# Mamba-2 stage: the masked B·C product held in PSUM, small sums in the banks of the transposes, and one tile's state input made by VectorE

## The chip, the cores and the metric

The kernel runs on one core of a Trainium2 chip. The core has a matrix engine (PE, TensorE), three engines for element-wise work (DVE = VectorE, ACT = ScalarE, POOL = GpSimd), and a queue that issues the transfers (SP, SyncE). The engines run their own instruction streams in order, and wait for one another through semaphores. Matmuls write to PSUM, eight banks of 128 x 512 fp32; everything else lies in SBUF. The metric is the time of one execution on the device in microseconds (us), lower is better. Before the change three runs took 1116.57, 1116.24 and 1118.81 us, a median of 1116.57.

## What is computed

One step of a two-layer recurrent decoder, for a prompt of 512 tokens and for eight samples of one token each, with the same weights. Layer 0 joins gated DeltaNet and gated linear attention. Layer 1, the only one that the change touches, is a Mamba-2 SSD block: 32 heads of width 64 in 4 groups, each group with one B and one C row of 128 numbers a token.

```python
def odd_layer(h, conv_buf, s_ssd, pre_g, post_g, w_in, conv_w, conv_b, dt_bias, a_log, d_skip, norm_g, w_out):
    u = rmsnorm(h, pre_g)
    z, xbc, dt = _split(einsum('bld,de->ble', u, w_in), ODD_SPLITS)
    xbc, new_buf = causal_conv(xbc, conv_buf, conv_w, conv_b)
    xs, Bm, Cm = _split(xbc, (SSD_DI, SSD_G * SSD_N, SSD_G * SSD_N))
    dt = softplus(dt + dt_bias)
    y, s_new = ssd_chunked(xs, dt, -exp(a_log), Bm, Cm, s_ssd)
    y = (y + d_skip[:, None] * xs) * silu(z)
    y = rmsnorm(y in 4 groups of 512, norm_g)
    return h + rmsnorm(y @ w_out, post_g), new_buf, s_new

def ssd_chunked(x, dt, A, Bm, Cm, h0):
    xdt, lam = x * dt[..., None], cumsum(dt * A)           # within a chunk
    m = einsum('nbtgs,nbjgs->nbgtj', Cm, Bm) * exp(lam_t - lam_j)   # for j <= t, else 0
    y = einsum('nbgktj,nbjgkp->nbtgkp', m, xdt) + exp(lam_t) * (C . state)
    state = exp(lam_last) * state + sum_j exp(lam_last - lam_j) * B_j x xdt_j
```

## The kernel before

**Stages.** The program computes layer 0, its output projection, the SSD block (from about 690 to 1050 us of the profiled execution) and its output projection. The Python code is a list of operations in the order of the algorithm; a scheduler deals them anew to each engine by its own model of their times, so the order in which an engine runs them isn't that of the text, and a small edit can move many rows. Tiles come from pools with a fixed number of buffers by tag: a new tile waits until the readers of the tile that had its buffer are done. Each PSUM tag has its own banks: pj 2, po 1, pf 1, pr 2, px 1, ps 1, eight in all. `bank(tag)` (L128) hands them out.

**A group of the SSD block** (`ssd_group`, four calls) has the same steps each time. All arrays are transposed: 128 features on the partitions, 512 tokens in four chunks of 128 along the free axis.

- B and C are projected (matmuls L267 to L269, three to a product because fp32 is split in two parts) and convolved (`conv`, DVE's products `stt`, L148, in bank pf). B is transposed by PE (L1232, a pr bank) and copied by ACT to `btk`, a tile of tag kqg. The products of B and C of each chunk (L1237) go to bank po; DVE multiplies them with the triangular mask `tri` into `cbm`, another kqg tile (`tt`, L145, in the trace kqg<-po,tri).
- The samples' B and C rows are transposed (L1245, bank ps), copied by ACT, written to DRAM (`bd`) and broadcast from there over all partitions into four tiles of tag inv (in the trace inv<-bd). `bcv` (matmul L1259, bank ps) is B·C of each sample.
- For each of four tiles j (two heads): x and the gate are projected and convolved; x is transposed (L1321, a pr bank); x times dt is made from PSUM into `xdt`, by DVE for tiles 0 to 2 (ch<-pr,c) and by eight scalings of ACT (L1328) for tile 3; POOL multiplies that with the decay to the chunk's end, `xdc`, into `xd[j]`, the input of the state (ap<-ch,c). For each head ACT makes the decay matrix (L1343, L1344), and DVE multiplies it with `cbm` (dec<-dec,kqg). The matmuls L1348 make y of the tile from both.
- With the tiles go the samples: `sample_x` and `sample_state(j)`, in which POOL multiplies the state by the broadcast C and B (sb<-inv,st and sb<-inv,smh), DVE reduces (L1285) and adds, and ACT scales the state (L1290). The samples of the last group are kept until after the stage.
- The states of the four chunks (L1361, pr banks) need `btk` and all four `xd`. Then, for each tile, the state's share of y (L1390) is scaled by DVE in PSUM (po<-po,pre), added, and multiplied with the gate; ACT squares, POOL adds the squares into `acc`. PE sums them by column (L1402, bank ps), DVE reads these sums (L1404), POOL takes the power -0.5 (smc), PE broadcasts the result over the partitions (L1410, `rs`, bank ps), and four products of DVE (L148, of<-of,vhalf,ps) scale y with it.

**What sets the order around the change.** The bank ps, of which there is one, serves in turn L1245, L1259, the column sums L1402 and `rs` (L1410), and in groups 1 and 3 the sum in `sample_norm` (L1217). The two pr banks serve the transposes of B and x, the states, and half of the L1390 products. Bank po serves L1237, L1348 and the other half of L1390.

Of the kernel before, what the change touches and what calls it, by code (L numbers as in the profile page):

```python
# [14 lines left out]
MULT, ADD, SUB, MIN, MAX, POW = ALU.mult, ALU.add, ALU.subtract, ALU.min, ALU.max, ALU.pow  # L15

P = 128
# [7 lines left out]
C = 128  # L25
NC = TP // C
# [5 lines left out]
SG = 4  # L32
# [25 lines left out]
def kernel(  # L58
# [45 lines left out]
    act, dve, pool, pe = nc.scalar, nc.vector, nc.gpsimd, nc.tensor  # L104
# [12 lines left out]
    phase = [0]  # L117
# [3 lines left out]
    def sb(shape, dt=F32, tag="f1"):  # L121
        uid[0] += 1
        return wrk.tile(shape, dt, name=f"{tag}_{uid[0]}", tag=tag, bufs=BUFS[tag])

    def const(shape, name, dt=F32):
        return cst.tile(shape, dt, name=name)

    def bank(tag):  # L128
        uid[0] += 1
        if tag == "po":  # L130
            tag = ("po", "pf")[npo[0] % 2 if phase[0] < 2 else 0]
            npo[0] += 1
        return psm.tile([P, 512], F32, name=f"{tag}_{uid[0]}", tag=tag, bufs=PBUFS[tag])
# [4 lines left out]
    def c4(ap):  # L138
        return ap.rearrange("p (c t) -> p c t", c=NC)
# [4 lines left out]
    def tt(eng, out, a, b, op):  # L144
        eng.tensor_tensor(out, a, b, op=op)  # L145
# [4 lines left out]
    def chunk(c):  # L150
        return slice(c * C, (c + 1) * C)
# [215 lines left out]
    start = ExitStack()  # L367
# [28 lines left out]
    tri = tri1.unsqueeze(1).to_broadcast([P, NC, P])  # L396
# [131 lines left out]
    ps = bank("pr")  # L528
# [8 lines left out]
    ps = bank("pr")  # L537
# [650 lines left out]
    ps = bank("pr")  # L1188
    for c in range(NC):
        pe.transpose(ps[:, chunk(c)], sd[:, chunk(c)], ident)  # L1190
    dtl = lay1[:, 0:256].rearrange("p (c h) -> p c h", c=NC)
    act.activation(dtl, c4(ps)[:, :, 0:64], AF.Copy)
    lamc = dtl[:, :, 32:64]
    ps = bank("pr")
# [3 lines left out]
    xdc = sb([P, NC, SH], tag="c5")  # L1198
    act.activation(slast, pv, AF.Exp)
    tt(dve, xdc, pv, lamc, SUB)  # L1200
    act.activation(xdc, xdc, AF.Exp)
    tailo = sb([P, 11, 24], tag="tail")
    ysm = sb([P, 16, NS], tag="c5")
    zsm = sb([P, 16, NS], tag="c5")
# [20 lines left out]
    def ssd_group(g):  # L1225
# [3 lines left out]
        b_, c_ = bcm  # L1229
        ps = bank("pr")  # L1230
# [1 line left out]
            pe.transpose(ps[:, chunk(c)], b_[:, chunk(c)], ident)  # L1232
        btk = sb([P, NC, C], tag="kqg")
        act.activation(btk, c4(ps), AF.Copy)
        ps = bank("po")
        for c in range(NC):
            pe.matmul(ps[:, chunk(c)], b_[:, chunk(c)], c_[:, chunk(c)], start=True, stop=True)  # L1237
        cbm = sb([P, NC, C], tag="kqg")
        tt(dve, cbm, c4(ps), tri, MULT)

        bcs = sb([P, 2, NS], tag="sms")
        conv_samples(tailo, cvw[1], hpo, 16 + g, 2, 4, bcs)
        ps = bank("ps")
# [14 lines left out]
        ps = bank("ps")  # L1258
# [48 lines left out]
        yt, xd, gts = [], [], []  # L1307
        for j in range(4):
            pr = 4 * g + j
            h0 = 2 * pr  # L1310
            x_ = sb([P, T], tag="kq")
            gt = conv_gate(o_w_in[0], (O_X + pr * P, pr * P), u1, pr, cvw[1], hpo, tailo, x_, pr == 15)
            pool.tensor_copy(zsm[:, pr], gt[:, TP:T])
            gts.append(gt)
            if j % 2 == 1:
                sample_x(j // 2)
            if j > 1:
                samples(j - 2)
            ps = bank("pr")
            for c in range(NC):  # L1320
                pe.transpose(ps[:, chunk(c)], x_[:, chunk(c)], ident)  # L1321
            sh = [P, NC, 2, 64]
            xdt = sb([P, NC, 2, 64], tag="ch")
            px = ps.rearrange("p (c h e) -> p c h e", c=NC, h=2)
            na = 4 if j == 3 else 0
            for c in range(na):
                for hh in range(2):
                    act.activation(xdt[:, c, hh], px[:, c, hh], AF.Copy, scale=dtl[:, c, h0 + hh:h0 + hh + 1])  # L1328
            if na < NC:
                tt(dve, xdt[:, na:], px[:, na:], dtl[:, na:, h0:h0 + 2].unsqueeze(3).to_broadcast([P, NC - na, 2, 64]), MULT)  # L1330
            xd.append(sb([P, NC, P], tag="ap"))
            tt(pool, xd[j].rearrange("p c (h e) -> p c h e", h=2), xdt,
               xdc[:, :, h0:h0 + 2].unsqueeze(3).to_broadcast(sh), MULT)

            po = bank("po")
            rbs = []
            for hh in range(2):
                h = h0 + hh
                rb = sb([P, TP], tag="dec")
                rbs.append(rb)  # L1340
                dma(rb, ldr[h:h + 1, :].to_broadcast([P, TP]))
                for c in range(NC):
                    act.activation(rb[:, chunk(c)], rb[:, chunk(c)], AF.Relu, scale=-1.0, bias=lamc[:, c, h:h + 1])  # L1343
                act.activation(rb, rb, AF.Exp, scale=-1.0)  # L1344
                tt(dve, c4(rb), c4(rb), cbm, MULT)
            for c in range(NC):
                for hh in range(2):
                    pe.matmul(po[hh * 64:hh * 64 + 64, chunk(c)], xdt[:, c, hh, :], rbs[hh][:, chunk(c)], start=True, stop=True)  # L1348
            yt.append(sb([P, T], tag="of"))
            y = yt[j][:, 0:TP]  # L1350
            stt(y, x_[:, 0:TP], dcol[:, pr:pr + 1], po, MULT, ADD)
# [5 lines left out]
        h0 = 8 * g  # L1357
        for c in range(NC):
            ps = bank("pr")
# [3 lines left out]
            if c:  # L1363
                sh = [P, 8, 64]
# [40 lines left out]
        tt(pool, rc, rc, nhalf[:, 0:NC], POW)  # L1405
        dg = sb([P, NC, C], tag="dec")
        tt(dve, dg, ident.unsqueeze(1).to_broadcast([P, NC, C]), bc3(rc, C), MULT)
        rs = bank("ps")
        for c in range(NC):
            pe.matmul(rs[:, chunk(c)], ones, dg[:, c, :], start=True, stop=True)  # L1410
        for j in range(4):
# [60 lines left out]
```

## Time and profile before

| | |
|---|---|
| median of three runs | 1116.57 us |
| the profiled execution | 1120.96 us |
| its span, from first to last instruction | 1119.2 us |
| mean clock granted to TensorE | 0.972 of full speed |
| SSD stage | about 690 to 1050 us |

The profile is one execution, recorded by the hardware. Its span leaves out 1.8 us around the program. A group of instructions is named by its line, engine, operation and tiles (`dec<-dec,kqg` is a product written to a dec tile from a dec and a kqg tile), followed by shapes, the count, busy time, mean time of one, and the idle time of the engine ahead of it with what ended it. A row of the timeline has its start, its length, the engine, the line, the instruction, and in brackets the idle time ahead. A row of the view by stretches has, for each engine (PE, its weight loads PEld, DVE, ACT, POOL), the busy time and the number of instructions, then the granted clock, the share of the DMA engines and the bytes moved (GB/s).

### The profile page before, as it was taken

How to read it: one execution, taken by the hardware profiler on the slowest of the kernel's cores; microseconds unless marked ns; L12 is line 12 of the kernel's file. 1: busy time of each engine (PE TensorE's matmuls, PEld its weight loads, DVE VectorE, ACT ScalarE, POOL GpSimd, SP SyncE). 2: the span in 40 equal slices, each digit the busy share in tenths (PEclk: the TensorE clock that was granted, in tenths of full speed). 3: DMA queues.
4: the chain of work that ended last, by engine and by line, in shares of the span. 5: the costliest groups of instructions: out<-in, count | busy, mean ns of one | idle time of the engine just before them, and what ended most of it. 6: DMA issues, size and time to landing. Idle time of an engine off the chain costs nothing.

```text
span 1119.2 us, 23031 instructions
## 1 busy us (share of the span) xinstructions
PE 1048.8 (94%) x8900; PEld 1006.4 (90%) x8900; DVE 720.3 (64%) x1207; ACT 627.4 (56%) x1518; POOL 535.7 (48%) x701
## 2 busy tenths in 40 slices
PE   8999979999989989999889999998999999999997
PEld 7999979899989989889888988898998988989997
DVE  5798353655867754565645366698787688778543
ACT  5566445544444645546233465775686676775452
POOL 4034961304124377114435362386469477468632
PEclk8999999999999989989998999999999999999999
DMA  5234245622554424745563351755657556657632
GB/s 166 81 92 110 72 139 153 194 59 78 171 145 124 110 70 130 217 137 146 160 197 115 100 170 39 210 146 144 188 170 198 181 161 194 206 177 216 187 90 78
DMA packets 241732, 160.01 MB, mean 143 GB/s; under 512 B 21463, under 2 KB 221358, under 8 KB 241606
## 3 DMA queue, kind: packets, MB, share of 16 engines
q1 hardware_dynamic: 241622, 158.53, 48.9%
q8 instruction: 70, 1.15, 0.4%
q14 instruction: 40, 0.33, 0.1%
HBM read 127.05 MB, written 31.84 MB: 142 GB/s over the span
## 4 chain that ended last, share of the span: by engine, by line
PE 40%; DMA 17%; POOL 15%; DVE 13%; ACT 8%; issue 4%; SPq 2%; DVEq 0%; POOLq 0%; ACTq 0%
PE pj L267 9%; PE pj L268 9%; PE pj L269 9%; POOL sb L145 6%; POOL st L145 3%; ACT dec L1343 2%; DVE w L145 2%; DMA sb<-ud 2%; DMA st<-in_state_ssd_dram 2%; DMA out_dram<-st 2%; DVE f L148 1%; DMA pre<-ldr 1%; POOL w L145 1%; DMA inv<-bd 1%; PE px L268 1%
## 5 line engine op out<-in xcount | busy, mean ns | idle before, releaser
L267 PE MATMUL pj<-ua,w 128*128 128x256 f32 x776 | 228.3, 295 | 4.5 <-ACT ua L342 1.7
L269 PE MATMUL pj<-ua,w 128*128 128x256 f32 x776 | 226.9, 293 | 1.2 <-DVE w L145 1.2
L267 PE MATMUL pj<-ub,w 128*128 128x264 f32 x768 | 226.5, 295 | 1.4 <-ACT ub L342 0.9
L269 PE MATMUL pj<-ub,w 128*128 128x264 f32 x768 | 225.7, 294 | 0.0
L268 PE MATMUL pj<-ub,w 128*128 128x264 f32 x742 | 219.0, 295 | 0.0
L268 PE MATMUL pj<-ua,w 128*128 128x256 f32 x750 | 217.7, 291 | 0.0
L145 DVE TENSOR_TENSOR w<-raw,w 128x1024 fp32r<-128x1024 f32 x102 | 136.2, 1335 | 62.9 <-PE pj L268 33.9
L267 PEld LDWEIGHTS pj<-ua,w 128*128 128x128 f32 x776 | 151.3, 195 | 7.4 <-ACT ua L342 2.0
L251 ACT ACTIVATE w<-raw 128x1024 fp32r<-128x1024 f32 x123 | 130.0, 1057 | 46.9 <-DMA raw<-in_o_w_out_dram 11.1
L269 PEld LDWEIGHTS pj<-ua,w 128*128 128x128 f32 x776 | 151.5, 195 | 3.1 <-DVE w L145 1.4
L267 PEld LDWEIGHTS pj<-ub,w 128*128 128x128 f32 x768 | 148.2, 193 | 2.6 <-ACT ub L342 1.1
L269 PEld LDWEIGHTS pj<-ub,w 128*128 128x128 f32 x768 | 148.1, 193 | 1.8 <-issue 1.5
L268 PEld LDWEIGHTS pj<-ua,w 128*128 128x128 f32 x750 | 146.7, 196 | 0.2
L268 PEld LDWEIGHTS pj<-ub,w 128*128 128x128 f32 x742 | 143.3, 193 | 1.6 <-issue 1.1
L145 POOL TENSOR_TENSOR w<-raw,w 128x1024 fp32r<-128x1024 f32 x20 | 49.7, 2484 | 49.1 <-PE px L268 19.4
L145 POOL TENSOR_TENSOR sb<-inv,st 128x512 f32<-128x512 f32 x32 | 54.3, 1714 | 22.7 <-DMA inv<-bd 13.7
L148 DVE SCALAR_TENSOR_TENSOR pf<-xr,cvw,pf 128x512 f32<-128x512 f32 x72 | 54.0, 750 | 11.6 <-ACT pf L440 10.7
L148 DVE SCALAR_TENSOR_TENSOR f<-xr,cvw,f 128x512 f32<-128x512 f32 x72 | 57.6, 799 | 4.3 <-ACT f L440 3.6
L145 POOL TENSOR_TENSOR sms<-sms,sms 128x16 f32<-128x16 f32 (+2 forms) x56 | 22.1, 396 | 77.0 <-ACT sms L960 41.9
L1290 ACT ACTIVATE st<-st,c 128x128 f32<-128x128 f32 x128 | 41.1, 395 | 24.6 <-POOL sb L145 24.6
L439 ACT ACTIVATE xr<-pj 128x256 f32<-128x256 f32 (+1 forms) x72 | 27.3, 380 | 36.7 <-PE pj L269 36.5
L1343 ACT ACTIVATE dec<-dec,c 128x128 f32<-128x128 f32 x128 | 40.5, 390 | 9.8 <-DMA dec<-ldr 8.6
(600 smaller groups left out, 2819.5 us busy)
## 6 DMA issues: line engine op xcount, KB each, us to landing
raw<-in_e_w_in_dram SPq DMA_DIRECT2D x56, 512.0 KB
raw<-in_o_w_in_dram SPq DMA_DIRECT2D x40, 512.0 KB
out_dram<-st SPq DMA_DIRECT2D x32, 512.0 KB
raw<-in_e_w_out_dram SPq DMA_DIRECT2D x32, 256.0 KB
st<-in_state_ssd_dram SPq DMA_DIRECT2D x16, 512.0 KB
dec<-ldr SPq DMA_DIRECT2D x32, 256.0 KB
raw<-in_o_w_out_dram SPq DMA_DIRECT2D x32, 256.0 KB
sb<-vd SPq DMA_DIRECT2D x8, 512.0 KB
```

The costliest lines, as they stand in the source:

```text
L145: eng.tensor_tensor(out, a, b, op=op)
L148: dve.scalar_tensor_tensor(out, a, s, b, op0=op0, op1=op1)
L251: act.activation(wh, rv, AF.Copy)
L267: pe.matmul(ps, wh, uh[b], start=(k == 0), stop=False)
L268: pe.matmul(ps, wh, ul[b], start=False, stop=False)
L269: i0 = pe.matmul(ps, wl, uh[b], start=False, stop=(k == NK - 1))
L439: act.activation(hsl(xr[:, 3:3 + T], b), halves[b], AF.Copy)
L1290: act.activation(st[:, b], st[:, b], AF.Copy, scale=sc2[:, 1, pr, b:b + 1])
L1343: act.activation(rb[:, chunk(c)], rb[:, chunk(c)], AF.Relu, scale=-1.0, bias=lamc[:, c, h:h + 1])
```

## The change

Four edits, all within the SSD stage.

1. `cbm` stays in PSUM. The products of B and C are written to bank ps, through a new tag "pc", and masked in place by DVE; bank po and one kqg tile are no longer used for it, and the mask products dec<-dec,cbm read one operand from PSUM.
2. Everything in the stage that asked for bank ps (L1245, L1259, the column sums L1402, the sum of `sample_norm`) now takes a pr bank.
3. `rs`, the broadcast of the norm, is put into bank po.
4. `xdl`, dt times `xdc` for heads 6 and 7 of each group, is made once by POOL; the state input of tile 3 is made by DVE from the transposed x in PSUM and `xdl`, instead of by POOL from `xdt` and `xdc`. ACT's eight scalings stay, since y needs `xdt`.

```diff
     def bank(tag):
         uid[0] += 1
+        if tag == "ps" and phase[0] == 2:
+            tag = "pr"
+        if tag == "pc":
+            tag = "ps"
...
     act.activation(xdc, xdc, AF.Exp)
+    xdl = const([P, NC, 8], "xdl")
+    tt(pool, xdl.rearrange("p c (g h) -> p c g h", g=SG), xdc.rearrange("p c (g h) -> p c g h", g=SG)[:, :, :, 6:8],
+       dtl[:, :, 0:32].rearrange("p c (g h) -> p c g h", g=SG)[:, :, :, 6:8], MULT)
...
-        ps = bank("po")
-        for c in range(NC):
-            pe.matmul(ps[:, chunk(c)], b_[:, chunk(c)], c_[:, chunk(c)], start=True, stop=True)
-        cbm = sb([P, NC, C], tag="kqg")
-        tt(dve, cbm, c4(ps), tri, MULT)
+        cbm = c4(bank("pc"))
+        for c in range(NC):
+            pe.matmul(cbm[:, c, :], b_[:, chunk(c)], c_[:, chunk(c)], start=True, stop=True)
+        tt(dve, cbm, cbm, tri, MULT)
...
-            tt(pool, xd[j].rearrange("p c (h e) -> p c h e", h=2), xdt,
-               xdc[:, :, h0:h0 + 2].unsqueeze(3).to_broadcast(sh), MULT)
+            if j == 3:
+                tt(dve, xd[j].rearrange("p c (h e) -> p c h e", h=2), px,
+                   xdl[:, :, 2 * g:2 * g + 2].unsqueeze(3).to_broadcast(sh), MULT)
+            else:
+                tt(pool, xd[j].rearrange("p c (h e) -> p c h e", h=2), xdt,
+                   xdc[:, :, h0:h0 + 2].unsqueeze(3).to_broadcast(sh), MULT)
...
-        rs = bank("ps")
+        rs = bank("po")
```

The scheduler deals the rows anew. Three places show how; the changed program's line numbers are 4 higher up to L1199 (L267 becomes L271), and 6 to 10 higher in the group's code (L1245 becomes L1251, L1321 becomes L1327, L1402 becomes L1412, L1410 becomes L1420).

On PE in group 1, the transposes of the samples' B and C rows (sms; the pj rows around them are matmuls of a projection) stand here before:

```order
L267 MATMUL pj_10338<-ub_8245,w_10309 128x264
L268 MATMUL pj_10338<-ub_8247,w_10309 128x264
L1245 MATMUL ps_9935<-ident,sms_9927 8x128 x2
L269 MATMUL pj_10338<-ub_8245,w_10310 128x264
L267 MATMUL pj_10338<-ub_8249,w_10309 128x264
```

And now, with `bcv` (L1265) right behind them:

```order
L273 MATMUL px_10225<-ub_8237,w_10197 128x264
L1251 MATMUL pr_9935<-ident,sms_9927 8x128 x2
L271 MATMUL px_10225<-ub_8241,w_10196 128x264
L272 MATMUL px_10225<-ub_8243,w_10196 128x264
L273 MATMUL px_10225<-ub_8241,w_10197 128x264
L1265 MATMUL pr_9953<-sms_9951,ones 128x8
L271 MATMUL px_10225<-ub_8245,w_10196 128x264
```

They write a pr bank, and have moved from a later projection (pj_10338) into an earlier one (px_10225): matmul 5632 of PE's queue before, 5567 now. In groups 2 and 3 they move from 6237 to 6185 and from 6815 to 6764.

On PE in group 0 the same transposes move the other way. Before they stand in the projection pj_8954:

```order
L269 MATMUL pj_8954<-ua_8232,w_8950 128x256
L267 MATMUL pj_8954<-ua_8236,w_8950 128x256
L1245 MATMUL ps_8856<-ident,sms_8848 8x128 x2
L268 MATMUL pj_8954<-ua_8238,w_8950 128x256
L269 MATMUL pj_8954<-ua_8236,w_8951 128x256
```

Now they stand in the projection px_9122:

```order
L271 MATMUL px_9122<-ua_8236,w_9118 128x256
L1251 MATMUL pr_8857<-ident,sms_8849 8x128 x2
L272 MATMUL px_9122<-ua_8238,w_9118 128x256
L1265 MATMUL pr_8875<-sms_8873,ones 128x8
L273 MATMUL px_9122<-ua_8236,w_9119 128x256
```

They are matmul 4966 of the queue instead of 4857, behind the transposes of dt (L1190) and of B, which use the pr banks too.

On DVE, the end of group 0's tiles, with the convolution of B of group 1 (pf), the reduction and the sum of a sample's state (smh, st), and y of tile 3 (of). Before:

```order
L1285 TENSOR_REDUCE smh_8879<-sb_9640 128x8
L148 SCALAR_TENSOR_TENSOR pf_9835<-xr_320,cvw_438,pf_9835 128x512
L145 TENSOR_TENSOR st_9638<-st_9638,sb_9644 128x1024
L148 SCALAR_TENSOR_TENSOR pf_9835<-xr_320,cvw_438,pf_9835 128x512 x2
L148 SCALAR_TENSOR_TENSOR kq_9777<-f_1757_9843,pf_9835 128x512
L148 SCALAR_TENSOR_TENSOR of_9617<-kq_9413,dcol,po_9592 128x512
```

And now, with the new state input (ap<-pr,xdl) between the products of the convolution:

```order
L152 SCALAR_TENSOR_TENSOR pf_9836<-xr_320,cvw_438,pf_9836 128x512
L1291 TENSOR_REDUCE smh_8880<-sb_9641 128x8
L152 SCALAR_TENSOR_TENSOR pf_9836<-xr_320,cvw_438,pf_9836 128x512
L149 TENSOR_TENSOR ap_9591<-pr_9577,xdl 128x512
L152 SCALAR_TENSOR_TENSOR pf_9836<-xr_320,cvw_438,pf_9836 128x512
L152 SCALAR_TENSOR_TENSOR of_9618<-kq_9414,dcol,po_9593 128x512
L149 TENSOR_TENSOR st_9639<-st_9639,sb_9645 128x1024
L152 SCALAR_TENSOR_TENSOR kq_9778<-f_1756_9844,pf_9836 128x512
```

The product of the state input stands behind the reduction of the sample (now L1291), and y of tile 3 has moved ahead of the sum of the sample's state and of the convolution's last product.

## Prediction, made before the changed kernel was run

> **What bounds the kernel now.** The page's busy times come first.
>
> ```profile
> span 1119.2 us, 23031 instructions
> PE 1048.8 (94%) x8900; PEld 1006.4 (90%) x8900; DVE 720.3 (64%) x1207; ACT 627.4 (56%) x1518; POOL 535.7 (48%) x701
> ```
>
> The change leaves the count of matmuls as it is, so it can only win what PE waits. The view of busy time by stretches shows the Mamba stage, the only one that the change touches, and what follows it.
>
> ```profile
> 690.00:1050.00 360.00, 339.00 (x2844) 326.13 (x2845) 280.25 (x337) 248.59 (x632) 233.74 (x253) 1.00 0.63 184
> 1050.00:1119.20 69.20, 61.04 (x509) 59.93 (x507) 28.46 (x51) 30.75 (x69) 26.08 (x32) 0.97 0.28 89
> ```
>
> Of 360 us PE is busy for 339 (the first pair of numbers), so at most 21 us are to be had; 339 us over 2844 records is 0.12 us a matmul, the measure by which I turn places in PE's queue into time. DVE is busy for 280, so it has little room. The waits of PE between 690 and 1055 us say what it waits for (total, times, longest).
>
> ```profile
> PE pr L1321 <- DVE kq L148: 6.5, 4, 2.1
> PE pr L1361 <- POOL ap L145: 3.8, 2, 3.3
> PE pj L267 <- ACT tail L441: 1.4, 1, 1.4
> PE po L1348 <- DVE ch L145: 1.4, 2, 1.2
> PE pj L267 <- ACT vg L1051: 1.3, 1, 1.3
> PE ps L1402 <- POOL ch L145: 1.3, 2, 1.0
> PE pj L269 <- DVE w L145: 1.2, 1, 1.2
> PE po L1348 <- ACT ch L1328: 1.2, 1, 1.2
> ```
>
> They sum to 18.1 us and are spread over four groups; six shorter ones are left out. No wait is long: PE is bound by its own work, with small holes where the convolutions (L1321), the state inputs (L1361) or the sums of squares (L1402) are late.
>
> **Part 1: the small sums leave the bank of the norm.** Before, the transposes of the samples' B and C rows (L1245) of group 1 take the one ps bank after the norm's broadcast (L1410) and the four products that read it:
>
> ```profile
> 798.21 0.84 POOL L145 TENSOR_TENSOR sms<-sms,sms 128x16 f32<-128x16 f32 x2
> 801.22 1.05 PE L1410 MATMUL ps<-dec,ones 128*128 128x128 f32 x8
> 804.98 2.72 DVE L148 SCALAR_TENSOR_TENSOR of<-of,vhalf,ps 128x512 f32<-128x512 f32 x4
> 808.16 0.38 PE L1245 MATMUL ps<-ident,sms 128*8 128x128 f32 x2
> 822.20 1.29 POOL L145 TENSOR_TENSOR sb<-inv,st 128x512 f32<-128x512 f32 x1 [5.39 <-DMA inv<-bd]
> ```
>
> The input is there at 799.05, the bank at 807.70, and L1245 runs at 808.16; the write to bd and the broadcasts to inv follow, and POOL idles 5.39 us for them. Over the stage:
>
> ```profile
> POOL sb L145 <- DMA inv<-bd: 13.7, 3, 5.4
> ```
>
> In the changed program L1245 stands 65, 52 and 51 matmuls earlier in groups 1, 2 and 3 (7.8, 6.2 and 6.1 us), since rs lies in po and the chain through pr asks only for the column sums' reader. The waits of groups 1 and 2 (5.4, and 2.9 as the rest of 13.7) should go. That is time of POOL; PE gets what stands behind the samples: L1348 1.4 + 1.2, L1402 1.3, L1361 0.5 (3.8 less 3.3), and L1321 3.5 in groups 2 and 3 (6.5 less the first group's two, 1.3 and 1.7, in rows of Part 2): 7.9 us. The bounds are nothing, if the order of DVE keeps each of them, and 7.9. I take half, **-4.0 us**: the lead of 6 to 8 us is longer than any of these waits, but PE's rows are dealt anew as well, and some ask for their input earlier.
>
> **Part 2: the fourth tile's state input.** In group 0 it costs PE 3.3 us (the last four rows; the first two, one from the list of waits between 700 and 720 us and one from the timeline, are the transposes of tiles 1 and 2 there):
>
> ```profile
> PE pr L1321 <- DVE kq L148: 1.3, 1, 1.3
> 750.92 0.66 PE L1321 MATMUL pr<-ident,kq 128*128 128x128 f32 x4 [1.70 <-DVE kq L148]
> 756.63 0.60 PE L1321 MATMUL pr<-ident,kq 128*128 128x128 f32 x4
> 764.02 1.69 ACT L1328 ACTIVATE ch<-pr,c 128x64 f32<-128x64 f32 x8
> 763.16 1.21 DVE L1285 TENSOR_REDUCE smh<-sb 128x8 f32<-128x1024 f32 x1
> 767.32 1.05 POOL L145 TENSOR_TENSOR ap<-ch,c 128x512 f32<-128x512 f32 x1
> ```
>
> POOL ends it at 768.37; ACT's eight scalings end at 765.71. The DVE product reads the same bank and in the program waits for ACT's last scaling; it takes about 0.69 us (rows below), so 766.4 is the earliest, 2.0 us sooner. Bounds: 3.3 (all of the wait) and nothing, if DVE is late, since it now stands behind a reduction that waits for POOL (the order shows it after L1285). I take **-2.0 us**, nearest to the row. It adds a wait on DVE: behind it stand the products of group 1's B convolution and y of tile 3, whose first use on PE, the B·C product, stands 122 matmuls, 14.6 us, behind tile 3's transposes.
>
> [...]
>
> **Part 3: the mask stays in PSUM.** The groups by line and shape of the stage (busy, mean ns of one, idle before), and the spread (min/median/max) of the first one:
>
> ```profile
> L145 DVE TENSOR_TENSOR dec<-dec,kqg 128x512 f32<-128x512 f32 x32 | 30.4, 951 | 8.0 <-ACT dec L1344 7.8
> L145 DVE TENSOR_TENSOR ch<-pr,c 128x512 f32<-128x512 f32 x12 | 8.2, 683 | 0.9 <-PE pr L1321 0.9
> L145 DVE TENSOR_TENSOR kqg<-po,tri 128x512 f32<-128x512 f32 x4 | 2.7, 685 | 0.2 <-PE po L1237 0.2
> L145 DVE TENSOR_TENSOR po<-po,pre 128x384 f32<-128x384 f32 x8 | 4.5, 557 | 0.4 <-PE po L1390 0.4
> L145 DVE TENSOR_TENSOR of<-of,po 128x384 f32<-128x384 f32 x8 | 4.4, 549 | 0.1
> L145 POOL TENSOR_TENSOR ap<-ch,c 128x512 f32<-128x512 f32 x16 | 16.8, 1050 | 5.0 <-DVE ch L145 4.4 <-PE pj L269 0.4 <-ACT ch L1328 0.2
> L145 DVE TENSOR_TENSOR dec<-dec,kqg x32: 680/692/2227, 711.1 to 992.4; 128x512 f32<-128x512 f32 x32
> ```
>
> The 32 mask products take 692 ns in the median but 951 in the mean: some lie up to 1.5 us longer beside POOL. Products with one operand in PSUM take 683 to 685 with no such excess. 32 x (951 - 685) = 8.5 us of DVE go; the mask's own product, now written in place, costs the same (557 against 549 for 384 columns); the four new state inputs add 4 x 0.685 = 2.7, and POOL loses 4 x 1.05 = 4.2 and gains one small product. DVE is 5.8 us lighter, 1.5 us a group. On PE's path this could shorten L1321, but in group 0 the transposes of tiles 1 and 2 now stand 56 and 72 matmuls earlier (6.7 and 8.6 us), which asks more than 1.5 us. I take **0**, between -3.0 (the two waits of group 0) and +3.0 (as much again).
>
> [...]
>
> **Part 4: what it costs.** In group 0 the chain through pr works the other way:
>
> ```profile
> 697.99 0.38 PE L1245 MATMUL ps<-ident,sms 128*8 128x128 f32 x2 [0.24 <-POOL sms L145]
> 711.40 3.79 POOL L145 TENSOR_TENSOR sb<-inv,st 128x512 f32<-128x512 f32 x2 [5.35 <-DMA inv<-bd]
> 728.43 2.04 POOL L145 TENSOR_TENSOR sb<-inv,smh 128x512 f32<-128x512 f32 x2
> 744.97 3.12 POOL L145 TENSOR_TENSOR sb<-inv,st 128x512 f32<-128x512 f32 x2 [3.56 <-DMA st<-in_state_ssd_dram]
> ```
>
> L1245 stands 109 matmuls later, 13.1 us, behind the transposes of dt and of B. Its writes and broadcasts move with it on SP, behind loads of weights. So 3.79 us of POOL's work leave a stretch in which it idled and come to stand at 728. The idle 3.56 at 744.97 should take most of it; bounds 0 and +3.8, I take **+0.5**. The next group's first transposes now wait, through pr, for the column sums of the group before; L1402 waited 1.0 at most: **+0.5**, between 0 and 1.3 a group. At the end POOL's order puts the samples' power ahead of the last two adds of squares:
>
> ```profile
> 1046.71 1.05 PE L1402 MATMUL ps<-ones,ch 128*128 128x1 f32 x8 [0.98 <-POOL ch L145]
> 1059.10 2.90 POOL L145 TENSOR_TENSOR sms<-sms,nhalf 128x16 f32<-128x16 f32 x1 [1.68 <-DVE sms L1217]
> ```
>
> 2.90 us and a small product more, but L1402 stands 38 matmuls (4.6 us) later: **0**, between -1.0 and +3.
>
> **The sum:** -4.0 - 2.0 + 0 + 0.5 + 0.5 = -5.0 us against the profiled execution's 1120.96, so 1115.96 there. That execution lies 4.39 us over the median of the three runs; the same difference from 1116.57 gives **1111.6 us**.
>
> **The rivals.** (a) *The holes close.* All of Part 1's 7.9, the 3.3 of Part 2 and the 3.0 of group 0 go: -14.2 + 1.0 = -13.2, 1103.4. For it speaks that the lead exceeds every wait; against it that PE's rows move too. (b) *It is hidden.* POOL is saved time in groups where it idles anyway, and the tail takes back what came before: in the stretch from 1005 to 1047 us
>
> ```profile
> 1005.00:1047.00 42.00, 39.63 (x326) 38.44 (x325) 30.23 (x29) 21.92 (x56) 37.22 (x29) 1.00 0.76 217
> ```
>
> POOL is busy for 37.22 of 42 us and L1402 waits for it at the end, so an earlier PE only waits longer there. What is left is Part 2 less Part 4: -1.0, 1115.6. (c) *Slower: group 0's samples lag.* The broadcasts come 13.1 us later; if the idle of 3.56 does not absorb POOL's 3.79 because the state's load lands no sooner, the lag goes on to tile 2's state input, to the samples' buffers and to each next group, and eats the gains: +3.8, 1120.4. It decides by when POOL's third pair of sample products ends in group 0, 748.09 before: if that comes later by the 3.79, nothing has absorbed them. (d) That the mask in PSUM doesn't speed DVE is inside the sum, since I take nothing for it.
>
> **How the numbers follow.** A measurement of this kernel tells about 0.3% (3.35 us) from no change: below 1113.2 is faster, above 1119.9 slower. The forecast has 0.46, (a) 0.12, (b) 0.23, (c) 0.19. So faster 0.58, same 0.23, slower 0.19. The likeliest case alone spans 1107.7 (all of Part 1, -3.9 more) to 1113.2. The range reaches past (a) by a little and to (c): 1102.0 to 1120.5.
>
> **What would show it.** Right: L1245 of group 1 about 7 us sooner after L1402's end and no wait of POOL for inv there; L1361 waiting under 1.5 us in group 0; the mask products near 690 ns with no long ones. Wrong: new waits of PE at L1321 on ACT's copies of the small rows, POOL idle over 10 us before its first sample product in group 0, DVE idle before the state input on ACT's scalings, or L1402 of the last group waiting more than 1 us.

## The result, and the profile after

The changed kernel took 1111.41 us (median of 22 runs) against 1117.51 us of the kernel before (22 runs): ratio 0.9944, 95% interval 0.9930 to 0.9958. The forecast was 1111.6 us. The size was met, by luck: the experiments below show that the way to it was another than the prediction's.

The head of the profile page after (span, busy times):

```profile
span 1115.3 us, 23031 instructions
PE 1052.9 (94%) x8900; PEld 1010.1 (91%) x8900; DVE 707.2 (63%) x1211; ACT 627.2 (56%) x1518; POOL 529.4 (47%) x698
```

DVE lost 13.1 us of work and POOL 6.3, and PE is busy 4.1 us longer, although it runs the same matmuls. The SSD stage by stretches of 90 us (length, then busy time and records of PE, PEld, DVE, ACT, POOL, granted clock, share of the DMA engines, GB/s), before:

```profile
690.00:780.00 90.00, 81.59 (x673) 78.41 (x674) 71.55 (x85) 63.99 (x164) 53.58 (x61) 0.98 0.59 164
780.00:870.00 90.00, 86.93 (x742) 84.23 (x741) 71.75 (x90) 62.92 (x157) 58.41 (x64) 1.00 0.62 181
870.00:960.00 90.00, 85.42 (x721) 81.84 (x720) 72.53 (x88) 62.86 (x160) 59.45 (x63) 1.00 0.61 181
960.00:1050.00 90.00, 85.07 (x715) 81.65 (x714) 64.41 (x76) 58.81 (x154) 62.31 (x66) 1.00 0.71 210
```

and after:

```profile
690.00:780.00 90.00, 87.67 (x743) 84.82 (x742) 74.18 (x97) 67.36 (x169) 50.82 (x61) 1.00 0.65 181
780.00:870.00 90.00, 87.78 (x737) 85.12 (x737) 69.18 (x87) 63.61 (x161) 64.26 (x67) 0.98 0.61 177
870.00:960.00 90.00, 86.27 (x720) 82.87 (x718) 67.49 (x88) 62.73 (x160) 57.06 (x66) 0.98 0.61 178
960.00:1050.00 90.00, 85.09 (x696) 81.14 (x697) 56.72 (x72) 56.30 (x148) 60.01 (x66) 0.98 0.67 202
```

PE's idle time is 90 us less its busy time: 8.4, 3.1, 4.6 and 4.9 us before, 2.3, 2.2, 3.7 and 4.9 after. Of the 7.8 us that went, 6.1 went in the first stretch, which holds group 0; the two next, where the prediction looked for its largest term, gave 1.7, and the last nothing. Not all of the 7.8 us is gain. A granted clock of 0.98 over 90 us is, in these traces, one piece of 3.4 us at half clock (rows in the next section), in which PE is busy longer for the same work, as an estimate by half of the 3.4, 1.7 us. Three stretches had such a piece after, one before. As an estimate, 7.8 less 2 x 1.7 is 4.4 us, and the two profiled executions lie 3.94 us apart (1120.96 and 1117.02).

The four largest waits of PE between 690 and 1055 us after (total, times, longest):

```profile
PE pr L1327 <- DVE kq L152: 3.5, 3, 2.4
PE pr L1412 <- POOL ch L149: 2.2, 2, 1.1
PE ps L1222 <- DVE sms L1220: 1.8, 1, 1.8
PE pr L1251 <- DVE c L149: 1.2, 1, 1.2
```

The transposes of x (L1327, before L1321: 6.5) wait 3.0 less, and no wait of the state (L1371, before L1361: 3.8) on POOL is left. New are short waits of the small sums: L1251 waits for its pr bank, L1222 is the sum in `sample_norm`.

### The profile page after: what moved, and what is told of

Same layout as the page of the kernel before. It is cut to its first block, busy times and chain, and to the rows that moved or that the text cites. A ratio compares the mean times of both kernels' runs of the same rounds, so it can differ in the third digit from the quotient of the medians.

```text
span 1115.3 us, 23031 instructions
## 1 busy us (share of the span) xinstructions
PE 1052.9 (94%) x8900; PEld 1010.1 (91%) x8900; DVE 707.2 (63%) x1211; ACT 627.2 (56%) x1518; POOL 529.4 (47%) x698
## 4 chain that ended last, share of the span: by engine, by line
PE 46%; POOL 16%; DMA 15%; DVE 12%; issue 5%; ACT 5%; SPq 1%; DVEq 0%; POOLq 0%; ACTq 0%
PE pj L271 10%; PE pj L272 10%; PE pj L273 10%; POOL sb L149 7%; POOL st L149 3%; PE px L272 2%; DMA sb<-ud 2%; POOL ap L149 1%; PE px L271 1%; PE px L273 1%; DVE w L149 1%; DMA st<-in_state_ssd_dram 1%; DVE f L152 1%; DMA dec<-odr 1%; ACT dec L1353 1%
## 5 line engine op out<-in xcount | busy, mean ns | idle before, releaser
L271 PE MATMUL pj<-ua,w 128*128 128x256 f32 x776 | 227.7, 294 | 1.3 <-ACT ua L346 0.7
L271 PE MATMUL pj<-ub,w 128*128 128x264 f32 x768 | 226.6, 295 | 1.6 <-ACT ub L346 1.1
L271 PEld LDWEIGHTS pj<-ua,w 128*128 128x128 f32 x776 | 151.4, 195 | 4.2 <-issue 1.9
L271 PEld LDWEIGHTS pj<-ub,w 128*128 128x128 f32 x768 | 148.0, 193 | 3.6 <-issue 1.3
L149 POOL TENSOR_TENSOR sb<-inv,st 128x512 f32<-128x512 f32 x32 | 46.9, 1482 | 21.4 <-DMA st<-in_state_ssd_dram 10.2
L149 POOL TENSOR_TENSOR sms<-sms,sms 128x16 f32<-128x16 f32 (+2 forms) x56 | 18.5, 332 | 71.0 <-ACT sms L964 42.0
L1353 ACT ACTIVATE dec<-dec,c 128x128 f32<-128x128 f32 x128 | 40.6, 391 | 10.4 <-DMA dec<-ldr 10.4
```

Source lines behind the costliest of these rows:

```text
L271: pe.matmul(ps, wh, uh[b], start=(k == 0), stop=False)
```

## Where the time in group 0 went

Six rows of group 0 before: DVE reduces the first sample, PE transposes x of tile 1, POOL makes two pairs of the samples' products and behind them the state input of tile 2, PE goes on with the states.

```profile
727.89 1.21 DVE L1285 TENSOR_REDUCE smh<-sb 128x8 f32<-128x1024 f32 x1
738.73 0.60 PE L1321 MATMUL pr<-ident,kq 128*128 128x128 f32 x4
754.85 2.55 POOL L145 TENSOR_TENSOR sb<-inv,smh 128x512 f32<-128x512 f32 x2
757.50 4.00 POOL L145 TENSOR_TENSOR sb<-inv,st 128x512 f32<-128x512 f32 x2
762.62 1.04 POOL L145 TENSOR_TENSOR ap<-ch,c 128x512 f32<-128x512 f32 x1
763.72 0.64 PE L1361 MATMUL pr<-ap,kqg 128*128 128x128 f32 x2 [3.29 <-POOL ap L145]
```

And after: POOL's first product of the samples, the transposes of tiles 1 and 2, the first sample's reduction, and the state.

```profile
728.21 1.30 POOL L149 TENSOR_TENSOR sb<-inv,st 128x512 f32<-128x512 f32 x1 [0.78 <-DMA inv<-bd]
729.78 0.60 PE L1327 MATMUL pr<-ident,kq 128*128 128x128 f32 x4
738.16 0.60 PE L1327 MATMUL pr<-ident,kq 128*128 128x128 f32 x4
733.77 1.21 DVE L1291 TENSOR_REDUCE smh<-sb 128x8 f32<-128x1024 f32 x1
742.42 2.03 POOL L149 TENSOR_TENSOR ap<-ch,c 128x512 f32<-128x512 f32 x1
760.88 0.68 DVE L149 TENSOR_TENSOR ap<-pr,xdl 128x512 f32<-128x512 f32 x1
761.61 1.38 PE L1371 MATMUL pr<-ap,kqg 128*128 128x128 f32 x10
```

The samples start 16.8 us later on POOL (728.21 against 711.40), and the prompt's tiles run ahead of them: tile 1 is transposed at 729.78 instead of 738.73, tile 2 at 738.16 instead of 750.92, and tile 2's state input starts at 742.42 instead of 762.62. Two things are to be read from the rows before. The wait of 3.29 us, which the prediction gave to tile 3's state input, ended at 763.72, when tile 2's was done (762.62 + 1.04 = 763.66); tile 3's ended only at 768.37. And the lag of group 0's samples, which the prediction priced as a cost, goes together with the gain.

The wait cost more than its own length. The stretches around it, before (PE is the first pair of numbers, the granted clock the third number from the end):

```profile
756.00:760.00 4.00, 4.00 (x40) 3.83 (x37) 2.82 (x3) 0.42 (x3) 4.00 (x5) 1.00 0.53 147
760.00:763.80 3.80, 0.51 (x5) 0.30 (x3) 3.80 (x4) 3.78 (x10) 3.80 (x4) 1.00 0.36 118
763.80:767.20 3.40, 3.40 (x16) 3.40 (x17) 2.74 (x4) 2.19 (x11) 3.32 (x5) 0.52 1.01 274
```

Behind the wait PE ran 3.4 us at half clock: 16 matmuls, against 40 in the 4 us ahead of it. After the change group 0 has neither the wait nor the slow piece. In the SSD stage of the 14 traces of this case there are 26 pieces at half clock, of 3.4 or 6.8 us, and in the 3.4 us ahead of each of them PE idled 0.9 to 3.4 us (3.2 before; 1.0, 2.3 and 1.9 in the change's trace, ahead of 791.03, 917.32 and 1033.38). The reverse doesn't hold: before, the wait of 2.06 us of L1321 that ends at 925.46 is followed by none, and the granted clock is 1.00 from 924.35 to 934. So the prediction's bound, that the change can win only the 21 us that PE waits, leaves out what a wait costs behind it.

## The experiments

Theory A is the prediction's sum. Theory B, from the trace after: the gain lies in group 0 and comes from the state input and the mask. C and D came up on the way. The runs are three series of four kernels, each beside the kernel before: rs in po alone, the state input alone, the banks, and the change without the state input; then the next four; then the last three and rs in po alone again. The whole change itself ran in a series of its own and in the second, not in the first and third.

**rs in bank po alone.** Part 1 by itself.

```diff
-        rs = bank("ps")
+        rs = bank("po")
```

> One edit of the change alone: the norm's broadcast rs goes to bank po, the other small sums stay in ps, mask and state input as before. The samples' transposes L1245 of groups 1 to 3 stand 69, 49 and 77 matmuls earlier, those of group 0 where they were. Theory A (the prediction's Part 1: the earlier broadcasts in groups 1 to 3 win most): 4 us faster than before, ratio about 0.9964, PE's idle time between 780 and 1050 us falls by about 4 of 12.6 us, and POOL no longer waits for inv in groups 1 and 2. Theory B (the trace after: PE's idle time fell by 6.1 of 7.8 us between 690 and 780 us, so the gain is in group 0, from the state input and the mask): within 1 us of before, ratio about 0.999, and the waits L1361 on POOL (3.3) and L1321 on DVE (1.3 and 1.7) in group 0 stay.

Measured: ratio 1.0046 (1.0028 to 1.0065), slower. Once more, on another chip:

> rs in bank po alone, once more on another chip: it was 5 us slower though the samples of groups 1 to 3 come 6 to 9 us earlier in PE's queue. If that holds, ratio 1.003 to 1.006; if it was chance of that chip, 0.998 to 1.001. Either way the prediction's -4.0 for this lead alone is refuted; 0.9965 would restore it.

Measured: 1.0018 (0.9994 to 1.0041). Group 1 in the timeline of the first of these runs:

```profile
796.80 0.38 PE L1245 MATMUL ps<-ident,sms 128*8 128x128 f32 x2
807.45 1.32 POOL L145 TENSOR_TENSOR sb<-inv,st 128x512 f32<-128x512 f32 x1 [5.50 <-DMA inv<-bd]
```

and from the list of POOL's waits in the stage:

```profile
POOL sb L145 <- DMA inv<-bd: 15.8, 3, 6.0
```

The lead is there: L1245 of group 1 at 796.80 instead of 808.16, the samples' product at 807.45 instead of 822.20. The wait of 5.4 us is still there too (5.50), 15 us earlier, and the three sum to 15.8 instead of 13.7. PE idled 8.65 us from 780 to 960, against 7.65 before. So the lead alone wins nothing, and theory A's largest term is refuted. Why the first of the two runs was slower was not followed.

**The state input on DVE alone.**

```diff
...
+            if j == 3:
+                tt(dve, xd[j].rearrange("p c (h e) -> p c h e", h=2), px,
+                   xdl[:, :, 2 * g:2 * g + 2].unsqueeze(3).to_broadcast(sh), MULT)
+            else:
...
```

> One edit alone: tile 3's state input by DVE out of PSUM; banks and mask as before. Theory A (the prediction's Part 2): 2 us faster, ratio 0.9982; L1361 in group 0 waits some 1.3 us instead of 3.3. Theory B: the whole wait of 3.3 us goes, L1361 waits under 0.5 us there, ratio about 0.997; the waits of L1321 in group 0 (1.3 and 1.7) stay, since the mask products still run long beside POOL. If DVE stands too late behind its reduction, L1361 waits as before and nothing is won.

Measured: 1.0003 (0.9985 to 1.0020). Waits of PE from 690 to 780 us:

```profile
PE pr L1324 <- DVE kq L148: 3.5, 3, 1.7
PE pr L1368 <- POOL ap L145: 2.7, 1, 2.7
```

The state (here L1368) still waits 2.7 us for POOL, although tile 3's input isn't POOL's any more. It waits for tile 2's, which POOL ends at 756.95; the state goes on at 757.00. Both theories had this wait fall with the edit, and both miss. The third case of the text above, that nothing is won, came, but not for its reason.

**Both moves of banks, without mask and state input.**

```diff
+        if tag == "ps" and phase[0] == 2:
+            tag = "pr"
...
-        rs = bank("ps")
+        rs = bank("po")
```

> Both moves of banks without mask and state input: small sums in pr, rs in po, the B.C product in po and copied to SBUF as before. Group 0's samples' transposes stand at matmul 4966 as in the whole change, and the transposes of tiles 1 and 2 stand at 5101 and 5169 (56 and 72 earlier than before). Theory A: 4.0 less 0.5 and 0.5, so 3 us faster, ratio 0.9973. Theory B: about 0, ratio 0.999 to 1.002: group 0's transposes of x come earlier in the queue while DVE still has its long mask products, so L1321 waits there for DVE as long as before (3.0 us) or longer, and L1361 still waits for POOL.

Measured: 0.9993 (0.9971 to 1.0016). In the trace PE idles 2.6 us from 690 to 780 instead of 8.4, with long mask products still on DVE (870 ns in the mean) and the state input on POOL, and no wait for POOL's input there is longer than 0.3. So it is the order that empties group 0 of idle time, neither the mask nor the state input: theory B is right on the place and wrong on the cause. Over all runs, though, that gave no time that can be told from nothing, although the interval just reaches theory A's 0.9973. A wait of 2.6 us of the state for POOL's input now stands in a later group.

**The whole change without the state input.**

```diff
-            if j == 3:
-                tt(dve, xd[j].rearrange("p c (h e) -> p c h e", h=2), px,
-                   xdl[:, :, 2 * g:2 * g + 2].unsqueeze(3).to_broadcast(sh), MULT)
-            else:
-                tt(pool, xd[j].rearrange("p c (h e) -> p c h e", h=2), xdt,
-                   xdc[:, :, h0:h0 + 2].unsqueeze(3).to_broadcast(sh), MULT)
+            tt(pool, xd[j].rearrange("p c (h e) -> p c h e", h=2), xdt,
+               xdc[:, :, h0:h0 + 2].unsqueeze(3).to_broadcast(sh), MULT)
```

> The whole change but for the state input, which stays on POOL: banks moved, mask in PSUM. Theory A: 3.0 us faster than before, ratio 0.9973 (the whole change less 2.0). Theory B: L1321 waits in group 0 go with the mask (3.0), L1361 waits for POOL again about 3.3 us there: ratio about 0.997 to 0.998, and the mask products take about 680 ns each, none over 700.

Measured: 0.9995 (0.9973 to 1.0018). Without the state input the gain is gone, while alone it was worth nothing. PE idles 2.2 us in the first stretch, as in the whole change, but 16.0 in the three others (10.9 after). Theory C was drawn from this: the parts pay only together. It compares runs of two series, which have only the kernel before in common.

**The whole change again**, beside the next three.

> The whole change once more, on the chip on which the parts below run. All theories: ratio 0.993 to 0.996 against before, as first measured. If it comes out at 0.998 or above, the gap between it and its parts was one of the chip and not of the edits.

Measured: 0.9948 (0.9926 to 0.9970). The gain holds.

**The whole change, mask copied to SBUF.**

```diff
-        cbm = c4(bank("pc"))
+        cbp = c4(bank("pc"))
+        cbm = sb([P, NC, C], tag="kqg")
...
-        tt(dve, cbm, cbm, tri, MULT)
+        tt(dve, cbm, cbp, tri, MULT)
```

> The whole change but for the mask: the masked product is written to an SBUF tile again (the product of B and C still in bank ps), so the mask products read two SBUF operands; banks moved, state input on DVE. First theory (the terms add; the mask is worth nothing): as the whole change, ratio 0.994 to 0.996, mask products 930 to 970 ns in the mean. Theory C (state input and mask only pay together, since DVE must be free when tile 3's transposed x is ready): ratio 0.998 to 1.000, like the change without the state input, and the DVE product of the state input starts later after the last scaling of ACT than in the whole change, with a wait of L1361 (here L1372) of 1 us or more in some group.

Measured: 0.9921 (0.9894 to 0.9948). The mask products after the change, in the groups by line and shape (busy, mean ns of one, idle before):

```profile
L149 DVE TENSOR_TENSOR dec<-dec,ps 128x512 f32<-128x512 f32 x32 | 21.6, 681 | 12.5 <-ACT dec L1354 12.4
```

and their spread (minimum, median, maximum in ns):

```profile
L149 DVE TENSOR_TENSOR dec<-dec,ps x32: 671/680/690, 712.9 to 986.4; 128x512 f32<-128x512 f32 x32
```

The same two views of this kernel:

```profile
L149 DVE TENSOR_TENSOR dec<-dec,kqg 128x512 f32<-128x512 f32 x32 | 32.1, 1012 | 10.4 <-ACT dec L1355 10.4
```

```profile
L149 DVE TENSOR_TENSOR dec<-dec,kqg x32: 675/708/2247, 705.1 to 976.8; 128x512 f32<-128x512 f32 x32
```

The mask in PSUM takes every long product away (maximum 690 ns instead of 2247) and spares DVE 10.5 us here. It wins no time: the kernel without it is no slower. Of the 10.5 us DVE spends 2.0 more waiting for ACT's decay matrices (12.4 us in the first row, 10.4 here); where the rest went was not followed. Theory C falls with this run, as far as it names the mask.

**rs in po and the state input**, group 0 in its old order.

```diff
-        rs = bank("ps")
+        rs = bank("po")
...
+            if j == 3:
+                tt(dve, xd[j].rearrange("p c (h e) -> p c h e", h=2), px, ...
```

> rs in bank po and the state input on DVE; the other small sums stay in ps and the masked product in SBUF. Group 0's samples' transposes stay at matmul 4857 and the transposes of tiles 1 and 2 at 5157 and 5241. First theory (terms add): 4.0 + 2.0 less nothing, ratio 0.995. Theory C: no gain, since rs alone was 5 us slower and the state input alone nothing: ratio 1.000 to 1.005, and group 0 keeps its waits L1321 (3 us and more) and most of L1361.

Measured: 0.9957 (0.9930 to 0.9984), faster, against theory C. Group 0 keeps 8.1 us of idle time, as expected, and the stage idles 20.5 us, hardly less than before. Its trace shows no gain in the stage at all: the same number of matmuls took 360.2 us there, against 359.6 before (table below). The part ahead of the stage, which the edits don't touch, took 683.4 us against 690.8. Whether the gain over all runs is the edit's stays open.

**Tile 3's gate product on DVE**, on top of the whole change.

```diff
-            tt(pool if j == 3 else dve, y, y, gt[:, 0:TP], MULT)
+            tt(dve, y, y, gt[:, 0:TP], MULT)
```

> The whole change, and the product of y with the gate of tile 3 goes from POOL to DVE, which the change has made about 6 us lighter in the stage. PE waits for POOL's last sum of squares at the column sums (1.0 and 1.1 us in groups 0 and 2). If POOL's chain of squares is what these wait for, both go and the kernel is 1 to 2 us faster than the whole change, ratio to before 0.992 to 0.9935; if DVE takes the place of POOL at the end of a group, it is the same or slower, 0.9945 to 0.997.

Measured: 0.9917 (0.9887 to 0.9947); its interval overlaps that of the whole change on the same chip, and PE still waits for POOL's squares at three column sums (2.0 us in all).

**Group 0's small sums back to their early place.** The whole change, but L1251 and L1265 of group 0 write to po.

```diff
-        ps = bank("ps")
+        ps = bank("po" if g == 0 else "ps")
```

> The whole change, but the two small sums of group 0 (the samples' transposes and bcv) go to bank po instead of pr. Group 0's samples then come early again (the transposes at matmul 4857, the transposes of tiles 1 and 2 at 5157 and 5241, as before the change); every place from group 1 on stays as in the whole change. Theory D (the gain of the banks is in group 0: samples that come later leave DVE and POOL to the prompt's tiles): PE's idle time in group 0 goes back from 3 or 4 us to 7.5 or more, with waits at L1327 and L1371, and the kernel is 3 to 4 us slower than the whole change, ratio to before 0.997 to 0.999. The prediction's Part 1 and Part 4 (the gain is in groups 1 to 3, and the lag of group 0's samples costs 0.5): 0.5 us faster than the whole change, ratio 0.994.

Measured: 0.9999 (0.9973 to 1.0025). This edit touches group 0's order only: in this trace and in that of the change, PE, DVE, ACT and POOL run the same instructions in the same order up to 697 us and from 764 us on (times of the change's trace). And the gain of 0.5% is gone. Group 0 in its timeline:

```profile
708.70 2.31 POOL L149 TENSOR_TENSOR sb<-inv,st 128x512 f32<-128x512 f32 x1 [5.85 <-DMA inv<-bd]
725.94 1.21 DVE L1291 TENSOR_REDUCE smh<-sb 128x8 f32<-128x1024 f32 x1
737.01 0.60 PE L1327 MATMUL pr<-ident,kq 128*128 128x128 f32 x4
747.53 0.66 PE L1327 MATMUL pr<-ident,kq 128*128 128x128 f32 x4
```

and from the list of PE's waits from 690 to 780 us:

```profile
PE pr L1371 <- POOL ap L149: 2.8, 1, 2.8
```

Samples early (708.70), tiles 1 and 2 late (737.01, 747.53), and the state waits 2.8 us for POOL again, with the mask in PSUM and the state input on DVE. PE idles 5.9 us in the first stretch, less than the 7.5 expected, and the time lies above the expected 0.997 to 0.999: theory D has the place and the sign, and both of its sizes miss.

The whole change didn't run beside this kernel, but the traces can be compared matmul by matmul. The 698 matmuls that hold everything that the edit moved (from 690.14 to 775.06 us in the change's trace) took 84.9 and 86.3 us in the two traces of the change, and 91.7 here; the 2146 behind them took 270.0, 267.0 and 268.5. So the loss, 5.4 to 6.8 us, lies within group 0. There PE idles 6.1 us against 2.3 and 3.6, and two waits, for L1327 and L1371, are each followed by 3.4 us at half clock (from 715.4 and 759.8); the change has no such piece there. That is 2.5 to 3.8 us of idle time and, as an estimate, 2 x 1.7 us of slower matmuls.

**Only group 0's small sums in pr.** The program before, with group 0's order of the whole change.

```diff
-        ps = bank("ps")
+        ps = bank("pr" if g == 0 else "ps")
```

> The program before, and only group 0's two small sums go from ps to pr; rs, mask and state input as before. Group 0's samples come later (matmul 4966, the transposes of tiles 1 and 2 at 5101 and 5169, as in the whole change); those of groups 1 to 3 get no lead (they stand 15, 75 and 88 matmuls later than before). Theory D: idle time of PE in group 0 falls from 7.7 to 3 or 4 us, 3 to 4 us faster than before, ratio 0.9965, less what the later samples of groups 2 and 3 give back. Prediction: 0.5 us slower in group 0, ratio 1.0005 or above.

Measured: 0.9999 (0.9973 to 1.0025). Its first and last stretch:

```profile
690.00:780.00 90.00, 86.32 (x737) 83.90 (x736) 73.15 (x93) 67.33 (x170) 55.95 (x60) 1.00 0.64 179
960.00:1050.00 90.00, 80.75 (x646) 77.01 (x646) 56.36 (x69) 54.67 (x146) 55.79 (x60) 0.96 0.70 208
```

Theory D's gain appears (idle 3.7 us instead of 8.4) and is given back at the end: 9.25 us idle in the last stretch instead of 4.9, where the samples' transposes stand 88 matmuls later.

**State input and gate on DVE, mask copied out.** Both edits on top of the whole change.

```diff
...
-        tt(dve, cbm, cbm, tri, MULT)
+        tt(dve, cbm, cbp, tri, MULT)
...
-            tt(pool if j == 3 else dve, y, y, gt[:, 0:TP], MULT)
+            tt(dve, y, y, gt[:, 0:TP], MULT)
```

> Banks moved, state input of tile 3 and its product with the gate on DVE, the masked product copied to SBUF: the parts that ran best. If mask and gate are worth what they gave apart (3 us each against the whole change): ratio 0.989. If both win by the same hole: 0.991 to 0.993, no better than either.

Measured: 0.9982 (0.9957 to 1.0008). Two versions that were 0.8% faster apart give nothing sure together, in another series on the same chip. No version beyond the change is shown to beat it.

The runs side by side. The idle time of PE is worked out from the stretches of one trace each. The last two columns count matmuls instead of us: the time of 698 matmuls of PE's queue, from the one at 690.14 us in the change's trace, which cover group 0 up to 775 us, and of the 2146 behind them, up to 1045 us.

| kernel | ratio to before | PE idle 690-780 | PE idle 690-1050 | group 0's 698 | next 2146 |
|---|---|---|---|---|---|
| before | 1 | 8.4 | 21.0 | 92.4 | 267.2 |
| whole change; again | 0.9944; 0.9948 | 2.3; 3.5 | 13.2; 16.4 | 84.9; 86.3 | 270.0; 267.0 |
| mask copied out | 0.9921 | 3.3 | 15.2 | 86.0 | 267.1 |
| gate on DVE too | 0.9917 | 3.4 | 17.3 | 86.2 | 267.3 |
| gate on DVE, mask copied out | 0.9982 | 2.8 | 16.7 | 85.7 | 272.1 |
| banks only | 0.9993 | 2.6 | 15.5 | 85.6 | 270.3 |
| no state input | 0.9995 | 2.2 | 18.2 | 86.1 | 275.9 |
| only group 0's sums in pr | 0.9999 | 3.7 | 18.4 | 86.3 | 273.8 |
| group 0's sums in po | 0.9999 | 5.9 | 20.4 | 91.7 | 268.5 |
| rs in po and state input | 0.9957 | 8.1 | 20.5 | 92.8 | 267.4 |
| state input only | 1.0003 | 7.9 | 17.6 | 92.6 | 264.2 |
| rs in po only; again | 1.0046; 1.0018 | 7.8; 6.8 | 20.6; 22.0 | 93.8; 92.6 | 269.1; 271.5 |

The column of group 0 falls in two: 84.9 to 86.3 us in the eight traces in which group 0's samples come late, 91.7 to 93.8 in the six in which they come early. In the last column the eight traces with the state input on DVE have 268.0 us in the mean (264.2 to 272.1), the six without it 271.3 (267.2 to 275.9); these ranges overlap, so that is a hint and no proof.

The count is the same in all kernels, though some instructions in it differ with the order. Less PE's idle time, and less half the length of the pieces at half clock, group 0's 698 take 82.0 to 82.8 us and the next 2146 take 253.4 to 255.7 in all 14 traces. So within the stage the kernels differ by PE's holes and the slow clock behind them, and hardly by PE's work.

## Why the prediction was right, and where it was not

The sum of -5.0 us was near the measured -6.1 because two wrong terms cancelled: the lead of the broadcasts in groups 1 to 3 is worth nothing alone, and the lag in group 0 is a gain. That the size came out is luck.

- **What bounds the kernel** was right: PE with small holes. The gain is in these holes and in the half clock that follows some of them (3.4 us behind the wait of 3.29 in group 0), which the prediction left out; DVE's busy time doesn't explain it, since its saving of 10 us in the mask products bought nothing.
- **Part 1 (-4.0) failed.** The step "that is time of POOL; PE gets what stands behind the samples" was wrong. The lead came as forecast, and alone it was not faster (1.0046, 1.0018). An earlier start alone moved POOL's wait for inv and didn't shorten it (5.39 us before, 5.50 with rs in po alone). After the change POOL still waits 3.35 us in group 1 before the samples' product at 802.15:

```profile
802.15 1.30 POOL L149 TENSOR_TENSOR sb<-inv,st 128x512 f32<-128x512 f32 x1 [3.35 <-DMA inv<-bd]
```

- **Part 2 (-2.0)** gave a wait to the wrong instruction: L1361 waited for tile 2's input, behind two pairs of sample products in POOL's queue. In group 0 the wait goes with the order (0.3 left with the banks alone) and stays with the state input alone (2.7). The prediction also read the waits of L1321 in group 0 one tile off: the one of 1.3 us ended at 716.77 and is that of tile 0, not of tile 1, whose transposes at 738.73 have no wait ahead of them. Within the whole change the state input is worth 0.5% all the same (0.9995 without it, 0.9944 and 0.9948 with it, in different series). The new wait on ACT's scalings was met once, 1.9 us in group 3, with no harm seen. What the edit buys was not found; the trace without it idles 3 to 5 us more after 780, spread over many short waits, and its 2146 matmuls behind group 0 took 275.9 us, against 270.0 and 267.0.
- **Part 3 (0)** was right, mechanism and worth: 951 ns became 681, 32 x 0.270 = 8.6 us of DVE against 8.5 forecast, and no time. Before, eight of the nine products over 1000 ns had POOL busy over their whole length (1002 to 2227 ns); the eight after the change of which the same holds took 671 to 689. The median is 680 ns with one operand in PSUM, and was 692 from SBUF before.
- **Part 4 (+0.5 for group 0's lag) had the wrong sign**, and so had rival (c), which made it the reason to be slower. Undoing only that lag took the gain away, and the loss lies in group 0 (91.7 us against 84.9 and 86.3). The sign that the prediction named for being wrong, POOL idle over 10 us ahead of group 0's samples, came (11.9 us in one piece, until DVE's part of a gate), and the time fell. What decided rival (c) spoke against it: POOL's third pair of sample products ended at 748.65 (746.09 + 2.56), against 748.09 before, so the lag was taken up by then. In group 0 no wait of PE for the samples is listed after the change, while before their products on POOL (754.85 and 757.50) stood ahead of tile 2's state input (762.62), in a queue that runs in order. The price of the later bank (+0.5) was not met as priced: L1412 waits 2.2 us for POOL's squares where L1402 waited 1.3, but no wait of the next group's transposes for the column sums is listed. The new waits of the samples' sums (L1222, 1.8 and 0.8 us) were in no term.
- **Rival (b)** came true in its outcome in one case, and not by its mechanism: with group 0's order alone, what group 0 won (6.1 us) the rest of the stage took back (6.6), but PE's longest wait in the last stretch is 3.4 us for a weight tile that POOL makes, not for the squares at the column sums.

What is shown: the lag of group 0's samples wins 5 to 9 us in group 0 in every trace that has it, and the change loses its gain without it. That the change also needs the state input rests on the time over all runs alone (0.9995 without it). Neither alone is measurably faster. What is open: by which waits the state input does its part, why the rest of the stage takes group 0's gain back in the kernels without it, and whether rs in po with the state input is faster in the stage at all. Another rival isn't ruled out for the ratios, that of the series: all four kernels of the second were faster than before by 0.4 to 0.8%, and none of the other two by more than 0.2%, although the last holds one (0.9982) that has all of the change but the mask. In the second series the changed kernels' mean granted clock was 0.978 to 0.980, that of the kernel before 0.976. The comparison within group 0 doesn't hang on this. Each of these edits makes the scheduler deal the rows anew, and one trace differs from the next of the same kernel by 3.2 us of idle time (13.2 and 16.4), so differences of that size in one trace are not explained.

## What to carry to other kernels

Work off the critical path can cost by its place in the queues that it shares: here an earlier start of it alone did not help the path (ratio 1.0046 and 1.0018), and a later one freed 5 to 9 us in group 0. Before a wait is priced, look at which instruction's end is the waiter's start: the row that ends at the same time, not the one that the edit touches. Where a scheduler deals the program anew, the parts of a change need not add (here 0.9921 and 0.9917 apart, 0.9982 together), and the test of a mechanism is an edit that moves one group and leaves every other place as it was. Two traces are then compared by the time between the same two matmuls, which leaves out what the rest of the run did.

## What the runs showed of the hardware

The mean granted clock differs from run to run of one kernel, and the time with it: in one series the kernel before took 1112.25 us at a mean clock of 0.983 and 1122.67 us at 0.971. A least-squares fit over 235 runs with their clocks, with a term for each kernel and series, gives 4.8 us (95%: 3.9 to 5.6) for 0.01 of the mean clock. Ahead of the SSD stage every kernel here runs the same instructions in the same order, and yet the 698 matmuls of group 0 begin at 682.3 to 690.8 us in the 14 traces. A difference of a few us between two single profiles is therefore no evidence before the clocks are compared.

Within the stage the clock falls to half for 3.4 or 6.8 us, in 26 cases over the 14 traces, and each time PE had idled 0.9 to 3.4 us of the 3.4 us ahead. So a hole in PE's work cost more than its length there: in group 0 before, 3.29 us of wait and, as an estimate, 1.7 us of slower matmuls behind it.
